# Strided attention on one Trainium2 core: output stored in runs of 2, 4, 4, 4, 4, 4 and 2 groups from one tile, and a TensorE loop of 24 groups

## The chip, the cores and the metric

One core of a Trainium2 chip. The metric is the device time of one execution in microseconds (us). The kernel before took 127.77 us, the median of three runs (127.75 to 128.23).

## What is computed

The inputs Q, K and V have 8 x 12 heads of 1024 positions with 64 numbers each, in float32. Every query attends to every 64th position only, which makes 16 keys and 16 values per head:

```python
attend_positions = np.arange(0, seq, stride)
k = K[:, :, attend_positions, :]
v = V[:, :, attend_positions, :]
scores = np.einsum('bhqd,bhkd->bhqk', q, k) * scale
weights = np.exp(scores - np.max(scores, axis=-1, keepdims=True))
weights = weights / (np.sum(weights, axis=-1, keepdims=True) + 1e-10)
result[:, :, i, :] = np.einsum('bhqk,bhkd->bhqd', weights, v)[:, :, 0, :]
```

Q comes in and the result goes out, 25.2 MB each; of K and V only 0.4 MB each are read.

## The kernel before, in words

The 96 heads are worked in 24 **groups** of four heads. One group is 1 MB of Q: 128 partitions of 8 KB. There are 18 buffers of that size in SBUF, `qn[0]` to `qn[17]`; group g uses `qn[g % 18]`, first for its queries and, once these are used up, for its result (the eviction writes the result over them). In the kernel before, two neighbouring buffers form one tile `pair`.

A group passes these steps, each on one engine:

- `load` (SyncE issues the DMA): Q into the group's buffer.
- `cast` (GpSimd, L305; the first three shared with ScalarE): float32 to bfloat16, into `qb`.
- `transpose` (VectorE, L316): 32x32 blocks of `qb` into `qt`.
- `scores` (TensorE, L324): 16 matmuls against the keys, into PSUM `sc`.
- `largest` (VectorE, L338 and L341): the maximum, and its subtraction, into `low`.
- `raise_` (ScalarE, L346): the exponential, into `ex`.
- `sums` (VectorE, L351 and L354): the sum over the 16 keys and its reciprocal.
- `weights` (GpSimd, L358): `ex` times the reciprocal, into `wt`.
- `turn` (TensorE, L365): four transposes of the weights, into PSUM `tp`.
- `spread` (ScalarE, L377, twice a group): `tp` into the block form `wb`.
- `outputs` (TensorE, L385): eight matmuls with the values, into PSUM `o`, of which there is one.
- `evict` (ScalarE, L403): `o` into the group's buffer.
- `store` (SyncE issues the DMA): the buffer to `out`.

All instructions are recorded first (class `Program`) and then written out in that order, each engine in its own strict order. The order is set by the list `ORDER` with a lag per step: in iteration i come `transpose` of group i, `cast` of i+1, `turn` and `spread` of i-3, `sums` and `weights` of i-2, `outputs` and `evict` of i-4, `largest` and `raise_` of i-1, `scores` of i, and the queue step for group i-5. On GpSimd, then, `cast(i+1)` stands ahead of `weights(i-2)`.

TensorE doesn't get its instructions one by one: it runs a loop of two groups per turn (`pe_stream`), in which step i does `scores(i)`, `turn(i-2)` and `outputs(i-3)`. Gates, semaphores that count up and are set back each turn, hold it: "turned" (VectorE's transposes), "weighted" (GpSimd's weights) and "free" (ScalarE's evictions). Before, the loop has 13 turns, so 26 steps for 24 groups; in the last two there are no more queries, VectorE opens the gate with a small memset (L314), and TensorE repeats score products that nobody reads. The last `outputs(23)` stands behind the loop.

SyncE issues every large DMA, on one hardware queue, and is itself in strict order: a wait at its head holds all that stands behind it. It first issues K, Q of group 0, V, and Q of groups 1 to 17. Then it follows `queue`: with each second group it issues one store of two groups and, at three of these points, the loads of two late groups (18 to 23), which go into buffers whose store must have landed. A store waits for ScalarE's count (`at_ACT`); a load into a used buffer waits for that buffer's store. Groups 22 and 23 are stored singly; the last store stands outside the recorded section, behind its closing handshake of the engines, and GpSimd waits meanwhile for the older stores and clears the semaphores.

The recorded section is opened by one engine, which tells the others to begin: before, SyncE.

Of the kernel before, what the change touches and what calls it, by code (L numbers as in the profile page):

```python
# [42 lines left out]
class Program:  # L43
# [89 lines left out]
    def emit(self, loop):  # L133
# [7 lines left out]
        gates = {name: nc.alloc_semaphore(f"gate_{name}") for name in names}  # L141
        with self.tc.tile_critical(no_gpsimd_drain=True):
# [26 lines left out]
def kernel(  # L169
# [21 lines left out]
    BUFS = 18  # L191
    RUN = 2
    assert NG % RUN == 0 and BUFS % RUN == 0

# [3 lines left out]
    edge = sb.tile([P, 32], FP32, name="edge")  # L198
    pairs = [sb.tile([P, RUN, 32 * D], FP32, name=f"pair{i}") for i in range(BUFS // RUN)]
    qn = [pairs[i // RUN][:, i % RUN] for i in range(BUFS)]  # L200
    k_raw = sb.tile([P, NC, D], FP32, name="k_raw")
# [108 lines left out]
    def transpose(g):  # L310
        k_in = {0: "0", 1: "1"}.get(g)
        words = qt[g % 2].bitcast(I32)
        if g >= NG:
            op("DVE", lambda: nc.vector.memset(edge[:, g - NG : g - NG + 1], 0.0), gate="turned")  # L314
            return
        op("DVE", lambda: nc.vector.transpose(  # L316
# [91 lines left out]
    def send(g, n):  # L408
        return _copy(
            nc,  # L410
            _ap_with(out, [[16 * D, P], [2 * SD, 2 * n], [1, 16 * D]], g * HG * SD),
            _ap_with(qn[g % BUFS], [pairs[0].ap[0], [1, 1], [1, 32 * n * D]]),
        )

    def store(g, n):
        op("SP", lambda: send(g, n), lane=f"out{g % BUFS // n}of{n}",
           reads=[f"qn{i % BUFS}{h}" for i in range(g, g + n) for h in range(2)])
# [33 lines left out]

    turns = (NG + 2) // TURN

    def queue(g):
        if g == NG - 2:
            store(g, 1)
        elif g % RUN == RUN - 1 and g < NG - 1:
            store(g - RUN + 1, RUN)
            late = BUFS + g - 2 * RUN + 1
            if BUFS <= late < NG:  # L460
                for n in range(late, late + RUN):
                    load(n)

    def at(i, stage, lag):
        g = i - lag
        if g in early.get(stage, ()):
            return
        if stage == "transpose" and 0 <= g < NG + 2:
            transpose(g)
        elif stage == "scores" and 0 <= g < NG + 2:  # L470
            scores(g)
# [25 lines left out]
    def pe_stream(sems, gates):  # L497
# [4 lines left out]
        with pe.Fori(0, turns) as turn_:  # L502
# [8 lines left out]
            for name in ("turned", "weighted", "free"):  # L511
                pe.sem_inc(gates[name], -TURN)

    pending, sems = prog.emit(pe_stream)
# [4 lines left out]
    tc.no_sync_barrier()  # L519
    end = send(NG - 1, 1)  # L520
    tc.declare_no_dep(end.ins, landed, reason="waits for the older stores alone")
# [33 lines left out]
```

## Time and profile before

| | us |
|---|---|
| median of three runs | 127.77 |
| the profiled execution's own time | 127.63 |
| its span, first to last instruction | 125.8 |
| ScalarE busy | 93.8 (75%) |
| VectorE busy | 87.1 (69%) |
| GpSimd busy | 75.9 (60%) |
| TensorE busy (matmuls) | 58.1 (46%) |
| bytes moved by DMA | 51.15 MB, mean 406 GB/s over the span |

The span leaves 1.8 us of the execution's own time outside it. Engines are named in the profile as PE (TensorE; PEld are its weight loads), DVE (VectorE), ACT (ScalarE), POOL (GpSimd) and SP (SyncE); SPq is SyncE's sequencer, which issues DMAs. A row of the timeline gives the start in us, the duration in us, engine, line, operation, output<-input and how many instructions are merged. "Landing" of a DMA is the time from its issue until the last of its 16 shares has landed.

### The profile page before, as it was taken

The page shows a single profiled execution, that of the slowest core. Times are in us where ns is not written, and L with a number is a line of the kernel's source. Part 1 is how long each engine was busy: PE and PEld are TensorE (multiplying, and loading weights), DVE is VectorE, ACT ScalarE, POOL GpSimd, SP SyncE. Part 2 cuts the span into 40 slices and gives each one's busy share as a digit, 9 for nine tenths or more (in the row PEclk, how much of TensorE's full clock was granted, in tenths as well). Part 3 has the DMA queues.
Part 4 walks back from the last instruction along what each step waited for, and adds up shares of the span by engine and source line. Part 5 has one row for each costly group of instructions (what it writes and reads, how often), then busy time and mean ns, then how long its engine had stood idle before and what let it go on. Part 6 is the DMA issues. An engine that isn't in the chain of part 4 may idle for free.

```text
span 125.8 us, 2084 instructions
## 1 busy us (share of the span) xinstructions
PE 58.1 (46%) x736; PEld 43.5 (35%) x736; DVE 87.1 (69%) x131; ACT 93.8 (75%) x109; POOL 75.9 (60%) x67
## 2 busy tenths in 40 slices
PE   0007672556489466665555565666656533000000
PEld 0006452445366444443443344444434321000000
DVE  3795879999979899999999999999966100000000
ACT  4266756999888999999999999999999965000000
POOL 5648589999998688889888888879233300000000
PEclk9999999998555999999999999999999975555555
DMA  1998989989899998999999999999999999999991
GB/s 41 425 406 385 490 365 479 448 385 479 365 479 437 406 469 354 422 422 479 417 391 458 422 385 432 464 406 424 417 422 422 427 427 437 427 432 417 406 424 65
DMA packets 6132, 51.15 MB, mean 406 GB/s; under 512 B 3696, under 2 KB 3696, under 8 KB 3696
## 3 DMA queue, kind: packets, MB, share of 16 engines
q1 hardware_dynamic: 6128, 51.12, 96.8%
q14 instruction: 4, 0.03, 0.1%
HBM read 25.95 MB, written 25.17 MB: 406 GB/s over the span
## 4 chain that ended last, share of the span: by engine, by line
ACT 51%; POOL 15%; DVE 7%; DMA 5%; PE 4%; issue 1%; SPq 1%; POOLq 0%
ACT pair L403 28%; ACT wb_all L377 16%; ACT ex L346 7%; POOL qb L305 6%; DMA v_raw<-in_V_dram 5%; POOL wt_all L358 4%; PE o L385 4%; POOL v_all L287 4%; DVE qt L316 3%; DVE total L351 1%; DVE top L338 1%; DVE rec L354 1%; POOL qb L301 1%; SPq L34 1%; DVE low L341 1%
## 5 line engine op out<-in xcount | busy, mean ns | idle before, releaser
L403 ACT COPY pair<-o 128x2048 f32<-128x2048 f32 x24 | 47.9, 1995 | 2.8 <-PE o L385 2.8
L305 POOL CAST qb<-pair 128x2048 bf16<-128x2048 f32 x21 | 39.7, 1892 | 1.5 <-DMA pair<-in_Q_dram 1.5
L385 PE MATMUL o<-v_all,wb_all 128*128 (+1 forms) x216 | 31.6, 295 | 8.2 <-ACT pair L403 8.2
L358 POOL TENSOR_TENSOR wt_all<-ex,rec 128x512 bf16<-128x512 f32 x24 | 25.4, 1058 | 15.4 <-DVE rec L354 15.1
L377 ACT ACTIVATE wb_all<-tp,sel 128x512 bf16<-128x512 bf16 x48 | 33.3, 810 | 0.7 <-PE tp L365 0.6
L316 DVE STREAM_TRANSPOSE qt<-qb 128x1024 int32<-128x1024 int32 x24 | 29.8, 1242 | 1.2 <-POOL qb L305 0.7
L385 PEld LDWEIGHTS o<-v_all,wb_all 128*128 128x128 bf16 x216 | 20.7, 105 | 14.9 <-issue 9.6
L324 PE MATMUL sc<-k_t,qt 128*128 x416 | 19.4, 200 | 12.9 <-DVE qt L316 12.8
L324 PEld LDWEIGHTS sc<-k_t,qt 128*128 128x128 bf16 x416 | 16.9, 103 | 17.5 <-issue 16.6
L365 PE MATMUL tp<-identity,wt_all 128*128 128x128 bf16 x104 | 11.1, 235 | 25.5 <-POOL wt_all L358 25.5
L346 ACT ACTIVATE ex<-low 128x512 f32<-128x512 f32 x24 | 18.3, 764 | 2.5 <-DVE low L341 2.5
L351 DVE TENSOR_REDUCE total<-ex 128x32 f32<-128x512 f32 x24 | 16.3, 678 | 3.9 <-ACT ex L346 3.9
L341 DVE TENSOR_TENSOR low<-sc,top 128x512 f32<-128x512 f32 x24 | 16.6, 691 | 0.8
L365 PEld LDWEIGHTS tp<-identity,wt_all 128*128 128x128 bf16 x104 | 6.4, 103 | 28.3 <-POOL wt_all L358 28.2
L338 DVE TENSOR_REDUCE top<-sc 128x32 f32<-128x512 f32 x24 | 15.2, 632 | 1.3 <-PE sc L324 1.3
L354 DVE RECIPROCAL rec<-total 128x32 f32<-128x32 f32 x24 | 8.5, 353 | 0.8
L287 POOL CAST v_all<-v_raw 32x128 bf16<-32x128 f32 (+1 forms) x12 | 5.2, 431 | 1.5 <-DMA v_raw<-in_V_dram 0.8
L299 ACT CAST qb<-pair 128x1024 bf16<-128x1024 f32 x3 | 3.1, 1045 | 3.1 <-DMA pair<-in_Q_dram 3.1
L301 POOL CAST qb<-pair 128x1024 bf16<-128x1024 f32 x3 | 3.1, 1039 | 3.3 <-DMA pair<-in_Q_dram 3.3
L259 POOL MEMSET v_all<- 128x3456 f32 x1 | 3.0, 2979 | 0.0
L287 ACT CAST v_all<-v_raw 32x640 bf16<-32x640 f32 x4 | 2.9, 722 | 0.0
L250 DVE MEMSET k_t<- 128x1664 uint32 x1 | 1.4, 1445 | 1.9 <-issue 1.9
(15 smaller groups left out, 9.6 us busy)
## 6 DMA issues: line engine op xcount, KB each, us to landing
pair<-in_Q_dram SPq DMA_DIRECT2D x24, 1024.0 KB, 15.0
out_dram<-pair SPq DMA_DIRECT2D x11, 2048.0 KB, 22.8
out_dram<-pair SPq DMA_DIRECT2D x2, 1024.0 KB, 18.7
k_raw<-in_K_dram SPq DMA_DIRECT2D x1, 384.0 KB, 3.9
v_raw<-in_V_dram SPq DMA_DIRECT2D x1, 384.0 KB, 6.8
```

Of the source, the lines that this page charges most:

```text
L305: op("POOL", lambda: nc.gpsimd.tensor_copy(out=b, in_=q), reads=[f"qn{g % BUFS}{h}" for h in range(2)] + apart, writes=[f"qb{g % 2}{h}" fo ...
L316: op("DVE", lambda: nc.vector.transpose(_ap_with(words, [words.ap[0], [1, 2], [D, 16], [2, 32]]), qb[g % 2].bitcast(I32),), reads=[f"qb{g ...
L324: r = nc.tensor.matmul(sc_ps[g % 2][:, 64 * i : 64 * i + 64], lhsT=_ap_with(qt[g % 2], [qt[g % 2].ap[0], [2, P]], extra_offset=2 * P * i + f),
L338: op("DVE", lambda: nc.vector.tensor_reduce(out=m, in_=s, op=ALU.max, axis=mybir.AxisListType.X,), reads=[f"sc{g % 2}"], writes=[f"top{g % ...
L341: op("DVE", lambda: nc.vector.tensor_tensor(out=low, in0=s, in1=m.unsqueeze(2).to_broadcast([P, 32, NK]), op=ALU.subtract,), reads=[f"sc{g ...
L346: op("ACT", lambda: nc.scalar.activation(out=ex[g % 2], in_=low, func=AF.Exp, bias=0.0, scale=scale,), reads=["low"], writes=[f"ex{g % 2}"])
L351: op("DVE", lambda: nc.vector.tensor_reduce(out=total[g % 2], in_=ex[g % 2], op=ALU.add, axis=mybir.AxisListType.X,), reads=[f"ex{g % 2}"] ...
L358: op("POOL", lambda: nc.gpsimd.tensor_tensor(out=wt[g % 2], in0=ex[g % 2], in1=rec[g % 2].unsqueeze(2).to_broadcast([P, 32, NK]), op=ALU.mult,
L365: r = nc.tensor.transpose(tp_ps[g % 2][:, 2 * c : 2 * c + 2].rearrange("p a b -> p (a b)"), wt[g % 2][:, 8 * c : 8 * c + 8].rearrange("p t ...
L377: op("ACT", lambda a=a: nc.scalar.activation(out=wb[g % 2][:, :, 64 * a : 64 * a + 64], in_=tp_ps[g % 2], func=AF.Copy, scale=sel[:, a : a ...
L385: r = nc.tensor.matmul(_ap_with(o_ps, [o_ps.ap[0], [128, 2], [256, 2], [1, D]], extra_offset=512 * c + D * u,), lhsT=wb[g % 2][:, 2 * c + ...
L403: op("ACT", lambda: nc.scalar.copy(to, o_ps.rearrange("p c (b x) -> p c b x", b=2)), reads=["o"], writes=[f"qn{g % BUFS}{n}" for n in rang ...
```

## The change

Four things are changed.

1. **Stores.** The 18 buffers become one tile `q_all`, and the stores are cut as the table `RUNS` says: groups 0-1, 2-5, 6-9, 10-13, 14-17, 18-21, and the last one, 22-23, behind the section. A store of n groups takes 8n KB from each partition, in pieces of 4 KB that lie 512 KB apart in `out`: 2n pieces, so four before and eight now.
2. **Late loads.** A load into a used buffer is now issued behind the first store of `RUNS` that comes after the one that frees it: 18 and 19 behind the store of 2-5, and 20 to 23 behind the store of 6-9.
3. **TensorE.** The loop has 12 turns; the last `turn` and `outputs` steps are written out behind it. The two idle memsets and the two repeats of score products (32 matmuls) are gone.
4. **The opening.** VectorE opens the recorded section.

```diff
-        with self.tc.tile_critical(no_gpsimd_drain=True):
+        with self.tc.tile_critical(sync_engine=mybir.EngineType.DVE, no_gpsimd_drain=True):
...
-    RUN = 2
-    assert NG % RUN == 0 and BUFS % RUN == 0
+    RUNS = {0: 2, 2: 4, 6: 4, 10: 4, 14: 4, 18: 4}
+    ENDS = {g + n - 1: (g, n) for g, n in RUNS.items()}
...
-    pairs = [sb.tile([P, RUN, 32 * D], FP32, name=f"pair{i}") for i in range(BUFS // RUN)]
-    qn = [pairs[i // RUN][:, i % RUN] for i in range(BUFS)]
+    q_all = sb.tile([P, BUFS, 32 * D], FP32, name="q_all")
+    qn = [q_all[:, i] for i in range(BUFS)]
...
-        if g >= NG:
-            op("DVE", lambda: nc.vector.memset(edge[:, g - NG : g - NG + 1], 0.0), gate="turned")
-            return
...
-    turns = (NG + 2) // TURN
+    turns = NG // TURN
+
+    late = list(range(BUFS, NG))
 
     def queue(g):
-        if g == NG - 2:
-            store(g, 1)
-        elif g % RUN == RUN - 1 and g < NG - 1:
-            store(g - RUN + 1, RUN)
-            late = BUFS + g - 2 * RUN + 1
-            if BUFS <= late < NG:
-                for n in range(late, late + RUN):
-                    load(n)
+        if g not in ENDS:
+            return
+        first, n = ENDS[g]
+        store(first, n)
+        while late and late[0] - BUFS < first:
+            load(late.pop(0))
...
             for name in ("turned", "weighted", "free"):
                 pe.sem_inc(gates[name], -TURN)
+        for j in range(2):
+            pe.wait_ge(gates["weighted"], j + 1)
+            turn_products(j).then_inc(done, 1)
+            pe.wait_ge(gates["free"], j + 1)
+            output_products(j + 1, NG + j).then_inc(done, 1)
...
-    end = send(NG - 1, 1)
+    end = send(NG - 2, 2)
```

SyncE's rows behind the first 20 DMAs, before. `pair0` holds groups 0 and 1 (later 18 and 19), `pair1` groups 2 and 3, `pair2` 4 and 5; `at_out0of2` counts the store of `pair0`.

```order
L34 DMA out_0_dram<-pair0_62 128x4x1024 [waits at_ACT]
L34 DMA out_0_dram<-pair1_63 128x4x1024 [waits at_ACT]
L34 DMA pair0_62<-in_Q_dram 128x2048 [waits at_out0of2]
L34 DMA pair0_62<-in_Q_dram 128x2048
L34 DMA out_0_dram<-pair2_64 128x4x1024 [waits at_ACT]
L34 DMA pair1_63<-in_Q_dram 128x2048 [waits at_out1of2]
L34 DMA pair1_63<-in_Q_dram 128x2048
L34 DMA out_0_dram<-pair3_65 128x4x1024 [waits at_ACT]
L34 DMA pair2_64<-in_Q_dram 128x2048 [waits at_out2of2]
L34 DMA pair2_64<-in_Q_dram 128x2048
```

The same place now, down to the section's end; `at_out0` counts the store of groups 0-1 and `at_out2` that of groups 2-5.

```order
L34 DMA out_0_dram<-q_all_62 128x4x1024 [waits at_ACT]
L34 DMA out_0_dram<-q_all_62 128x8x1024 [waits at_ACT]
L34 DMA q_all_62<-in_Q_dram 128x2048 [waits at_out0]
L34 DMA q_all_62<-in_Q_dram 128x2048
L34 DMA out_0_dram<-q_all_62 128x8x1024 [waits at_ACT]
L34 DMA q_all_62<-in_Q_dram 128x2048 [waits at_out2]
L34 DMA q_all_62<-in_Q_dram 128x2048 x3
L34 DMA out_0_dram<-q_all_62 128x8x1024 [waits at_ACT] x3
```

Ahead of load 20 now stand 10 groups of stores on the queue, where before there were 6; it waits for the store of groups 2-5, where before it waited for that of 2-3.

TensorE's rows at the end of the loop and behind it, before: the loop's last transposes and output products, the branch, and `outputs(23)`.

```order
L365 MATMUL tp1_97<-identity_79,wt_all_92 128x128 [waits gate_weighted]
L365 MATMUL tp1_97<-identity_79,wt_all_92 128x128 x3
L385 ISA [waits gate_free]
L385 MATMUL o_98<-v_all_82,wb_all_93 128x2x2x64 x8
L502 REGISTER_ALU
L502 COMPARE_AND_BRANCH
L385 MATMUL o_98<-v_all_82,wb_all_93 128x2x2x64 [waits at_ACT]
L385 MATMUL o_98<-v_all_82,wb_all_93 128x2x2x64 x7
```

And now: behind the branch stand `turn(22)`, `outputs(21)`, `turn(23)`, `outputs(22)` and `outputs(23)`.

```order
L499 REGISTER_ALU
L499 COMPARE_AND_BRANCH
L362 MATMUL tp0_88<-identity_71,wt_all_84 128x128 [waits gate_weighted]
L362 MATMUL tp0_88<-identity_71,wt_all_84 128x128 x3
L382 MATMUL o_90<-v_all_74,wb_all_85 128x2x2x64 [waits gate_free]
L382 MATMUL o_90<-v_all_74,wb_all_85 128x2x2x64 x7
L362 MATMUL tp1_89<-identity_71,wt_all_84 128x128 [waits gate_weighted]
L362 MATMUL tp1_89<-identity_71,wt_all_84 128x128 x3
L382 MATMUL o_90<-v_all_74,wb_all_85 128x2x2x64 [waits gate_free]
L382 MATMUL o_90<-v_all_74,wb_all_85 128x2x2x64 x7
L382 MATMUL o_90<-v_all_74,wb_all_85 128x2x2x64 [waits at_ACT]
L382 MATMUL o_90<-v_all_74,wb_all_85 128x2x2x64 x7
```

Each transposed or output step has the wait that it had in the loop; only the score products between them have left.

More of the change, by code (lines that the diff above doesn't have):

```diff
@@ L411, in send @@
             _ap_with(out, [[16 * D, P], [2 * SD, 2 * n], [1, 16 * D]], g * HG * SD),
-            _ap_with(qn[g % BUFS], [pairs[0].ap[0], [1, 1], [1, 32 * n * D]]),
+            _ap_with(qn[g % BUFS], [q_all.ap[0], [1, 1], [1, 32 * n * D]]),
         )
     def store(g, n):
-        op("SP", lambda: send(g, n), lane=f"out{g % BUFS // n}of{n}",
+        op("SP", lambda: send(g, n), lane=f"out{g % BUFS}",
            reads=[f"qn{i % BUFS}{h}" for i in range(g, g + n) for h in range(2)])
@@ L467, in at @@
             return
-        if stage == "transpose" and 0 <= g < NG + 2:
+        if stage == "transpose" and 0 <= g < NG:
             transpose(g)
-        elif stage == "scores" and 0 <= g < NG + 2:
+        elif stage == "scores" and 0 <= g < NG:
             scores(g)
```

## The prediction

> **What bounds the kernel now.** I read the page's slices first, then the queue's share, then windows by stage, then single DMAs.
>
> ```profile
> span 125.8 us, 2084 instructions
> ...
> ACT  4266756999888999999999999999999965000000
> ...
> DMA  1998989989899998999999999999999999999991
> ...
> q1 hardware_dynamic: 6128, 51.12, 96.8%
> ```
>
> ScalarE is full in the middle and has nothing to do in the last sixth; the DMA row is full from the second slice to the last but one. So the profile's chain of waits, which ends with ScalarE's evictions, tells what the compute is bound by, but compute isn't what the span waits for: the last eviction is over at 106.7 us (104.83 + 1.87, quoted below) and 18 us of stores are still queued. The windows show the rate, in their last two columns (share of the 16 DMA engines, GB/s):
>
> ```profile
> core 0: us, PE busy (x) PEld busy (x) DVE busy (x) ACT busy (x) POOL busy (x), PEclk, DMA share, GB/s
> 0.00:2.00 2.00, 0.00 (x0) 0.00 (x0) 0.10 (x1) 0.68 (x1) 0.57 (x6) 1.00 0.02 4
> 8.00:50.00 42.00, 26.17 (x324) 20.26 (x324) 37.11 (x54) 36.28 (x47) 35.71 (x35) 0.88 1.00 429
> 50.00:85.00 35.00, 20.47 (x280) 15.24 (x280) 34.27 (x52) 35.00 (x41) 29.16 (x21) 1.00 1.01 428
> 107.00:122.00 15.00, 0.00 (x0) 0.00 (x0) 0.00 (x0) 0.00 (x0) 0.00 (x0) 0.50 0.99 421
> 122.00:123.00 1.00, 0.00 (x0) 0.00 (x0) 0.00 (x0) 0.00 (x0) 0.00 (x0) 0.50 0.90 377
> 123.00:124.00 1.00, 0.00 (x0) 0.00 (x0) 0.00 (x0) 0.00 (x0) 0.00 (x0) 0.50 0.30 123
> ```
>
> From 8 to 122 us the engines have no idle time, with loads alone (8 to 50), mixed (50 to 85) or stores alone (107 to 122). The span is therefore the DMA's start (about 2 us), 51.12 MB at 421 to 429 GB/s, and a ragged end: from 122 to 124 the 16 engines stop at different times, over some 2 us. The forecast has to say what the change does to these three, and whether the queue ever runs dry.
>
> **The change part by part.** The sum is made against the profiled execution: 127.63 us, 1.8 us more than its span, and 0.14 below the median of 127.77.
>
> *The bytes* are the same. Only the store's shape can change the rate. Issue times (timeline) and landings (DMA view of the same moment; last number) of four stores and one late load:
>
> ```profile
> 29.60 0.63 SPq L34 DMA_DIRECT2D out_dram<-pair  x1
> out_dram<-pair SPq DMA_DIRECT2D x1, 2048.0 KB, 25.8
> 86.55 0.54 SPq L34 DMA_DIRECT2D out_dram<-pair  x1
> out_dram<-pair SPq DMA_DIRECT2D x1, 2048.0 KB, 23.8
> 100.38 0.54 SPq L34 DMA_DIRECT2D out_dram<-pair  x1
> out_dram<-pair SPq DMA_DIRECT2D x1, 2048.0 KB, 19.7
> 107.28 0.54 SPq L34 DMA_DIRECT2D out_dram<-pair  x1
> out_dram<-pair SPq DMA_DIRECT2D x1, 1024.0 KB, 17.8
> 60.72 0.47 SPq L34 DMA_DIRECT2D pair<-in_Q_dram  x1
> pair<-in_Q_dram SPq DMA_DIRECT2D x1, 1024.0 KB, 12.0
> ```
>
> The store issued at 86.55 lands at 110.35, the next but one (100.38) at 120.08: 9.73 us for two stores of 2 MB, 4.87 us each, which is 431 GB/s (2.097 MB / 4.87). That equals the loads' 429, so there is no fixed cost between queued stores for a larger one to save. A 4 MB store is not in this trace. Bounds: if five of them ran at 429 instead of the 421 of the last stage, 20.97 MB would take 48.9 instead of 49.8 us, a gain of 0.9; if the stores are no better than the neighbouring pair of 2 MB, 0. For a loss I know no reason but the pitch (below); the same 0.9 stands on that side for the range. I take a **gain of 0.2 us**, nearer to the pair of stores, since these are the direct neighbours.
>
> On the DMA's row pitch the Trainium skill speaks against this change: "DMA: Bandwidth & Descriptors", section "Latency and other measured facts", gives 207 GB/s for copies whose rows lie 512 KiB apart. The pieces of a store lie 512 KB apart here, four now and eight after. By that rule 25 MB of stores would already take over 120 us alone, and the trace has 421 to 431 GB/s, so the rule doesn't bind this pattern with four pieces; eight no run here shows yet.
>
> *The opening.* The chain of waits begins so (start, duration, what):
>
> ```profile
> 0.72 0.01 SPq L142
> ...
> 0.80 0.03 SPq L550
> ...
> 0.96 0.43 SPq L236
> ```
>
> SyncE tells the others at 0.72 to begin, passes its own branch at 0.80 and issues K at 0.96. If VectorE tells them instead, SyncE loses one instruction and gains a handover: between -0.08 (the whole step from 0.72 to 0.80) and +0.08. I take 0.
>
> *TensorE's tail* lies under the stores; one of the two repeats of score products that go:
>
> ```profile
> 97.34 0.63 PE L324 MATMUL sc<-k_t,qt 128*128 x16
> ```
>
> Before, the last eviction ends at 106.7, and the last store of 1 MB is issued 0.6 later, at 107.28, and lands at 125.08. At 107.28 the queue still holds the store issued at 100.38, which lands at 120.08; the 32 matmuls and two memsets that go cost nothing while that is so. Without this cover such a step would cost 0.63 us, and both 1.3.
>
> *The late loads* are the part that moves most. Walk along the queue by landings, 4.87 us for 2 MB and 2.44 for a load (1.049 MB at 429): the store of groups 0-1 lands at 55.4 (29.60 + 25.8) as now. Then come the store of 2-5 (9.74: 65.1), loads 18 and 19 (70.0), the store of 6-9 (79.8) and load 20 (82.2). The same walk for the kernel before gives 55.4 + 4.87 + 4.88 + 4.87 + 2.44 = 72.5, and the trace has 72.7 (60.72 + 12.0), so I set load 20 at **82.5**, 21 to 23 at 85, 87.4 and 89.8. GpSimd wants it earlier:
>
> ```profile
> 74.95 1.89 POOL L305 CAST qb<-pair 128x2048 bf16<-128x2048 f32 x1
> 77.39 1.06 POOL L358 TENSOR_TENSOR wt_all<-ex,rec 128x512 bf16<-128x512 f32 x1 [0.55 <-DVE rec L354]
> ...
> 78.50 0.40 PE L365 MATMUL tp<-identity,wt_all 128*128 128x128 bf16 x4 [1.19 <-POOL wt_all L358]
> ...
> 79.64 1.15 ACT wb_all L377 x2
> 80.80 1.75 ACT pair L403
> ...
> 84.24 1.76 ACT pair L403
> ```
>
> `cast(20)` starts at 74.95 now; its load would come 7.6 us later. Behind it in GpSimd's order waits `weights(17)` (77.39), for that `turn(17)` (78.50), and for that `spread(17)` (79.64). Starting cast at 82.55, weights follow at 84.4, turn at 85.5, spread at 85.95: ScalarE, which is otherwise full at 3.44 us a group (80.80 to 84.24), loses **6.3 us**. It can't win them back; the other late loads come 2.4 us apart and are then early enough. So the last eviction ends at 106.7 + 6.3 = 113.0 and the last store is issued at 113.6.
>
> Does that dry the queue? The store of 14-17 needs `evict(17)`, over at 92.3 (84.24 + 1.76 + 6.3), and the queue comes to it at 99.3 (load 23 at 89.5 by the walk, plus 9.74). The store of 18-21 is released where today the store of 20-21 is, at 100.38, plus 6.3: **106.7**. It is wanted when the store of 14-17 ends: 109.0. From issue to first byte it is about 1.1 us (K: issued at 0.96, no bytes but 4 GB/s before 2.00), so bytes flow at 107.8. The 109.0 is the slowest engine's; the ragged end says that the earliest are up to some 2 us ahead, so a few may idle for under 1 us. That shortens only their lead, not the slowest engine's work. The last store (113.6 against 109.0 + 9.74 = 118.7) has 5 us in hand. Cost: **0**, with the margin of 1.2 us against the slowest engine.
>
> Sum: 127.63 - 0.2 + 0 + 0 + 0 = 127.4; set beside the median, which is 0.14 higher, I forecast **127.5 us**.
>
> **The rivals.**
>
> *The queue runs dry ahead of groups 18-21 (slower).* TensorE's clock is the piece that can do it. These rows show half clock (the third number from the end) and what output products then take:
>
> ```profile
> 30.83:41.07 10.24, 7.69 (x74) 5.75 (x70) 8.79 (x13) 9.01 (x10) 9.55 (x9) 0.50 1.04 445
> ...
> 33.50 1.91 PE L385 MATMUL o<-v_all,wb_all 128*128 x8
> ...
> 75.80 1.04 PE L385 MATMUL o<-v_all,wb_all 128*128 x8 [0.35 <-ACT pair L403]
> ...
> 35.45 1.87 ACT L403 COPY pair<-o 128x2048 f32<-128x2048 f32 x1 [0.44 <-PE o L385]
> ...
> 39.38 1.87 ACT L403 COPY pair<-o 128x2048 f32<-128x2048 f32 x1 [0.38 <-PE o L385]
> ...
> 104.83 1.87 ACT L403 COPY pair<-o 128x2048 f32<-128x2048 f32 x1 [1.98 <-PE o L385]
> ```
>
> Output products take 1.91 instead of 1.04 us, and evictions come 3.93 us apart (35.45 to 39.38) instead of 3.44. TensorE would stand idle from 77.3 (78.50 less the 1.19 in its row) to 85.5 while load 20 is late. If it resumes at half clock, the first group loses 0.9 and the next two 0.5 each: up to 1.9 us, and the store of 18-21 is released at 108.6, with bytes at 109.7, against 109.0. That is 0.7 us late for the slowest engine. With load 20 another 0.5 late, 1.2: **128.1 to 128.6** (127.4 plus the loss). It decides from a ScalarE delay of 7.5 us (6.3 + 1.2). For it: the idle time is sure. Against it: the margin and the raggedness.
>
> The Trainium skill, "TensorE: Matmul & The Clock Gate", section "What's actually happening", has the clock halved after an idle window of about 3.4 us and restored after a busy one. The 10.24 us at 0.50 above are three such windows, in a stretch that was far from idle, so the trace agrees on the size of the steps but not on idleness as the only cause. By that rule the clock would be halved here.
>
> *Larger stores are better than I take (faster).* The whole 0.9 of the bound, or a less ragged end: half of the 2 us between 122 and 124. That gives **126.5 to 127.0**. Against it: 4.87 us for 2 MB is already the loads' rate.
>
> *A fixed cost per DMA is saved.* If every DMA cost the 1.1 us that K takes from issue to first byte, six DMAs fewer would save 6.6: **120.8**. The rows contradict it: stores queued behind one another land 4.87 us apart at the loads' rate, with nothing between them. I give it 1 in 100. The Trainium skill's page on DMA, section "Anatomy of one DMA — SWDGE (gpsimd) path", fits 2.0 us per DMA on another issuing path; by that it would be 12 us and 115.4.
>
> *It doesn't do what it says:* if a store of four groups is handled as two of two, nothing changes but the late loads, **127.6**, inside the forecast.
>
> **How the numbers follow.** Forecast, with the last rival in it: 0.66. Queue dry, or the eight pieces slower by the 0.9 (128.5): 0.20. Larger stores or an evener end: 0.13. Fixed cost: 0.01. A change of 0.5% (0.64 us of 127.77) is about what a measurement of this kernel can tell from none: below 127.13 counts as faster, above 128.41 as slower. Of the 0.20, 0.07 stay below 128.41, and of the 0.13, 0.02 above 127.13. So faster 0.12, same 0.75, slower 0.13. The range for 8 in 10 runs from 126.8, most of the gain's bound, to 128.6, the far end of the dry queue.
>
> **What would show it.** Right: DMA share about 1.00 in every stage up to 122 us; load 20 landing at 82 to 83 us; GpSimd idle about 5 us ahead of a cast, ended by a DMA; ScalarE's last eviction ending near 113; neighbouring 4 MB stores landing 9.7 us apart. Wrong: a window between 106 and 111 us with the DMA share well below 1.00 and the end later by as much (the dry queue); 4 MB stores landing 9.5 or 9.9 us apart (their rate); a first load's issue that moved by more than 0.1 us (the opening).

## The result, and the profile after

The kernel after takes **129.17 us**, the median of five runs (128.81 to 129.60), against 127.95 us for the kernel before on the same chip (127.75 to 128.23): **1.010 times as long, 95% interval 1.008 to 1.012**. That is slower than the 127.5 us forecast and outside the forecast's range. Times, ratios and counts here leave disturbed executions out.

Each execution has a time and a span. For the kernel before, over 137 executions beside these experiments, the mean span is 126.10 us, and the time is 1.72 to 1.85 us more (mean 1.78). For the five executions of the kernel after, the mean span is 127.04, and the time is 1.76 to 2.60 more (mean 2.17). So some 0.9 us were lost inside the span and 0.4 us outside. The profiled execution took 129.6 us.

From the page after: the span, TensorE's clock and the DMA engines in 40 slices (3.2 us each), the queue's share, the chain's shares by engine, and the row of GpSimd's casts, with its idle time last.

```profile
span 127.5 us, 1998 instructions
...
PEclk9999999997569999999999999755555595555555
DMA  1999999989999999999999999999999999299795
...
q1 hardware_dynamic: 5264, 51.12, 95.5%
...
DMA 36%; ACT 20%; POOL 14%; PE 13%; DVE 6%; issue 2%; SPq 1%; POOLq 0%; DVEq 0%
...
L305 POOL CAST qb<-q_all 128x2048 bf16<-128x2048 f32 x21 | 39.7, 1891 | 10.1 <-DMA q_all<-in_Q_dram 10.0
```

The row of the casts before:

```profile
L305 POOL CAST qb<-pair 128x2048 bf16<-128x2048 f32 x21 | 39.7, 1892 | 1.5 <-DMA pair<-in_Q_dram 1.5
```

The same bytes as before, but the row of DMA has a hole (the 2) in the slice from 108 to 112 us, the casts wait 10.0 us for loads instead of 1.5, and the clock is at half from the middle of the wait (81.6 us) until long behind it. The windows show the hole (columns as in the prediction; bytes are counted where their transfer starts):

```profile
core 0: us, PE busy (x) PEld busy (x) DVE busy (x) ACT busy (x) POOL busy (x), PEclk, DMA share, GB/s
81.60:102.00 20.40, 13.48 (x116) 10.11 (x116) 13.69 (x20) 13.36 (x15) 12.60 (x9) 0.50 1.01 429
85.00:107.00 22.00, 16.06 (x134) 11.82 (x135) 16.54 (x25) 18.36 (x22) 12.12 (x10) 0.58 1.01 429
107.00:122.00 15.00, 5.20 (x24) 2.70 (x22) 0.47 (x2) 7.31 (x6) 1.06 (x1) 0.50 0.82 351
108.00:109.00 1.00, 0.31 (x4) 0.31 (x4) 0.00 (x0) 1.00 (x1) 0.64 (x1) 0.50 0.31 131
109.00:110.00 1.00, 0.54 (x5) 0.21 (x4) 0.00 (x0) 1.00 (x2) 0.00 (x0) 0.50 0.08 33
110.00:111.00 1.00, 1.00 (x6) 0.71 (x5) 0.00 (x0) 0.88 (x2) 0.00 (x0) 0.50 0.00 0
111.00:112.00 1.00, 0.65 (x4) 0.15 (x1) 0.00 (x0) 0.31 (x1) 0.00 (x0) 0.50 1.21 524
```

Up to 107 us the queue is as full as before. Then the engines run out one by one, from 110 to 111 nothing starts, and between 111.5 and 111.7 all 16 start together, each with 32 KB, which takes it 1.2 us. (A second without a start is no proof by itself: once the engines run in step, a full queue has such seconds too, 119 to 120 for one. The hole is read from the three seconds from 108 to 111 together.) The timeline tells where that comes from (start, duration, engine, what, and in brackets the idle time ahead and what ended it):

```profile
66.00 2.61 SPq L34 DMA_DIRECT2D q_all<-in_Q_dram  x4
...
73.64 1.06 POOL L355 TENSOR_TENSOR wt_all<-ex,rec 128x512 bf16<-128x512 f32 x1 [0.40 <-DVE rec L351]
83.46 1.89 POOL L305 CAST qb<-q_all 128x2048 bf16<-128x2048 f32 x1 [8.76 <-DMA q_all<-in_Q_dram]
85.31 1.06 POOL L355 TENSOR_TENSOR wt_all<-ex,rec 128x512 bf16<-128x512 f32 x1
86.42 0.61 PE L362 MATMUL tp<-identity,wt_all 128*128 128x128 bf16 x4 [9.40 <-POOL wt_all L355]
87.07 1.26 ACT L374 ACTIVATE wb_all<-tp,sel 128x512 bf16<-128x512 bf16 x2 [7.73 <-PE tp L362]
88.77 1.87 ACT L400 COPY q_all<-o 128x2048 f32<-128x2048 f32 x1 [0.44 <-PE o L382]
92.71 1.86 ACT L400 COPY q_all<-o 128x2048 f32<-128x2048 f32 x1 [0.38 <-PE o L382]
...
107.84 1.86 ACT L400 COPY q_all<-o 128x2048 f32<-128x2048 f32 x1 [0.30 <-PE o L382]
110.32 0.54 SPq L34 DMA_DIRECT2D out_dram<-q_all  x1
115.54 1.86 ACT L400 COPY q_all<-o 128x2048 f32<-128x2048 f32 x1 [1.98 <-PE o L382]
```

Load 20, issued at 66.00, lands 17.3 us later, at 83.3 (first row of the next fence). `cast(20)` has waited 8.76 us for it, TensorE 9.40 for the weights behind it, ScalarE 7.73. TensorE resumes at half clock, and the evictions, which before came 3.44 us apart, come 3.94 apart at first. `evict(21)` starts at 107.84 and the store of groups 18 to 21 is issued at 110.32: 9.94 us after the 100.38 of before. By then the store ahead of it, of 14 to 17, issued at 95.13, is at its end (DMA view of the moment of each issue; the last number is the landing):

```profile
q_all<-in_Q_dram SPq DMA_DIRECT2D x1, 1024.0 KB, 17.3
...
out_dram<-q_all SPq DMA_DIRECT2D x1, 4096.0 KB, 15.7
...
out_dram<-q_all SPq DMA_DIRECT2D x1, 4096.0 KB, 11.6
```

95.13 + 15.7 = 110.8, and the store behind it starts to move at 111.5 and lands at 110.32 + 11.6 = 121.9: the queue was dry, for 0.7 us even on the slowest of its 16 engines.

### The profile page after: what moved, and what is told of

Read it like the earlier page. It is cut to its first block, busy times and chain, and to the rows that moved or that the text cites. A ratio compares the mean times of both kernels' runs of the same rounds, so it can differ in the third digit from the quotient of the medians.

```text
span 127.5 us, 1998 instructions
## 1 busy us (share of the span) xinstructions
PE 64.9 (51%) x704; PEld 48.2 (38%) x704; DVE 87.2 (68%) x129; ACT 94.4 (74%) x109; POOL 75.9 (59%) x67
## 3 DMA queue, kind: packets, MB, share of 16 engines
q1 hardware_dynamic: 5264, 51.12, 95.5%
## 4 chain that ended last, share of the span: by engine, by line
DMA 36%; ACT 20%; POOL 14%; PE 13%; DVE 6%; issue 2%; SPq 1%; POOLq 0%; DVEq 0%
DMA out_dram<-q_all 16%; ACT q_all L400 16%; DMA q_all<-in_Q_dram 14%; PE o L382 12%; POOL qb L305 6%; DMA v_raw<-in_V_dram 5%; POOL wt_all L355 4%; POOL v_all L287 3%; DVE qt L313 3%; ACT wb_all L374 3%; ACT ex L343 2%; DVE total L348 1%; PE tp L362 1%; DVE top L335 1%; DVE rec L351 1%
## 5 line engine op out<-in xcount | busy, mean ns | idle before, releaser
L400 ACT COPY q_all<-o 128x2048 f32<-128x2048 f32 x24 | 46.5, 1938 | 5.1 <-PE o L382 5.1
L305 POOL CAST qb<-q_all 128x2048 bf16<-128x2048 f32 x21 | 39.7, 1891 | 10.1 <-DMA q_all<-in_Q_dram 10.0
L382 PE MATMUL o<-v_all,wb_all 128*128 (+1 forms) x216 | 37.6, 333 | 9.1 <-ACT q_all L400 9.1
L374 ACT ACTIVATE wb_all<-tp,sel 128x512 bf16<-128x512 bf16 x48 | 31.9, 752 | 9.1 <-PE tp L362 9.0
L382 PEld LDWEIGHTS o<-v_all,wb_all 128*128 128x128 bf16 x216 | 23.4, 117 | 18.4 <-issue 9.6
L362 PE MATMUL tp<-identity,wt_all 128*128 128x128 bf16 x104 | 12.6, 256 | 30.1 <-POOL wt_all L355 30.1
L321 PEld LDWEIGHTS sc<-k_t,qt 128*128 128x128 bf16 x384 | 18.2, 111 | 15.2 <-issue 13.8
L343 ACT ACTIVATE ex<-low 128x512 f32<-128x512 f32 x24 | 17.2, 718 | 2.1 <-DVE low L338 2.0
L301 POOL CAST qb<-q_all 128x1024 bf16<-128x1024 f32 x3 | 3.1, 1037 | 3.9 <-DMA q_all<-in_Q_dram 3.9
L299 ACT CAST qb<-q_all 128x1024 bf16<-128x1024 f32 x3 | 3.1, 1045 | 2.4 <-DMA q_all<-in_Q_dram 2.3
```

Source lines behind the costliest of these rows:

```text
L305: op("POOL", lambda: nc.gpsimd.tensor_copy(out=b, in_=q), reads=[f"qn{g % BUFS}{h}" for h in range(2)] + apart, writes=[f"qb{g % 2}{h}" fo ...
L321: r = nc.tensor.matmul(sc_ps[g % 2][:, 64 * i : 64 * i + 64], lhsT=_ap_with(qt[g % 2], [qt[g % 2].ap[0], [2, P]], extra_offset=2 * P * i + f),
L343: op("ACT", lambda: nc.scalar.activation(out=ex[g % 2], in_=low, func=AF.Exp, bias=0.0, scale=scale,), reads=["low"], writes=[f"ex{g % 2}"])
L362: r = nc.tensor.transpose(tp_ps[g % 2][:, 2 * c : 2 * c + 2].rearrange("p a b -> p (a b)"), wt[g % 2][:, 8 * c : 8 * c + 8].rearrange("p t ...
L374: op("ACT", lambda a=a: nc.scalar.activation(out=wb[g % 2][:, :, 64 * a : 64 * a + 64], in_=tp_ps[g % 2], func=AF.Copy, scale=sel[:, a : a ...
L382: r = nc.tensor.matmul(_ap_with(o_ps, [o_ps.ap[0], [128, 2], [256, 2], [1, D]], extra_offset=512 * c + D * u,), lhsT=wb[g % 2][:, 2 * c + ...
```

## The experiments

Theory A: the late load dries the queue, by ScalarE's delay and TensorE's half clock together; nothing else costs. Rivals: the 4 MB stores are slower in themselves; the new tail or the opening costs something. All runs at a glance; the ratio is to the kernel before on the same chip, spans and "outside" (time minus span) are means in us, and the last column counts the executions with 2.4 us or more outside:

| run | what it is | ratio, 95% interval | span | outside | 2.4 or more |
|---|---|---|---|---|---|
| before | | 1 | 126.10 | 1.78 | 0 of 137 |
| after | | 1.010 (1.008 to 1.012) | 127.04 | 2.17 | 2 of 5 |
| e11 | after, SyncE opens | 1.0121 (1.0087 to 1.0154) | 127.33 | 2.33 | 4 of 6 |
| e1 | after, loads 20-23 earlier | 1.0053 (1.003 to 1.0076) | 126.38 | 2.21 | 5 of 11 |
| e2 | after, store 18-21 in pairs | 1.0056 (1.0035 to 1.0077) | 126.51 | 2.09 | 4 of 12 |
| e3 | after, TensorE kept busy, straight code | 1.0214 (1.0171 to 1.0257) | 128.84 | 1.77 | 0 of 5 |
| e6 | after, TensorE kept busy, loop | 1.0043 (1.0023 to 1.0062) | 126.63 | 1.80 | 0 of 7 |
| e7 | e1, all stores of 2 MB | 1.0031 (1.0005 to 1.0057) | 125.99 | 2.19 | 5 of 12 |
| e4 | before, late loads as after | 1.001 (0.9999 to 1.0021) | 126.23 | 1.77 | 0 of 12 |
| e8 | before, stores of 1 MB | 1.0132 (1.0115 to 1.015) | 127.67 | 1.82 | 0 of 3 |
| e5 | before, new tail and opening | 1.004 (1.0009 to 1.0072) | 126.17 | 2.17 | 5 of 12 |
| e9 | before, new opening | 1.0013 (0.9988 to 1.0038) | 126.38 | 1.77 | 0 of 12 |
| e10 | before, new tail | 1.0041 (1.0018 to 1.0064) | 126.20 | 2.21 | 5 of 12 |
| e12 | after, old loop | 1.0044 (1.0027 to 1.0061) | 126.66 | 1.78 | 0 of 10 |
| e13 | before, last turn straight | 1.0023 (1.0008 to 1.0039) | 126.25 | 1.82 | 0 of 12 |
| e14 | before, new tail as a loop | 1.0008 (0.9992 to 1.0024) | 126.03 | 1.90 | 0 of 12 |
| e15 | e1, old loop | 1.0034 (1.0012 to 1.0056) | 126.38 | 1.78 | 0 of 12 |
| e16 | after, tail as a loop | 1.003 (1.0002 to 1.0059) | 126.61 | 1.82 | 0 of 12 |
| e17 | e10, padded | 1.0009 (0.9995 to 1.0022) | 126.21 | 1.79 | 0 of 12 |
| e18 | e7, tail as a loop | 0.9998 (0.9983 to 1.0013) | 125.95 | 1.91 | 0 of 12 |

### The dry queue

**e1: loads 20 to 23 ahead of the store of 6 to 9.**

```diff
-        store(first, n)
+        if first == 2:
+            store(first, n)
         while late and late[0] - BUFS < first:
             load(late.pop(0))
+        if first != 2:
+            store(first, n)
```

> The changed kernel with one thing undone: loads 20 to 23 are issued ahead of the store of groups 6-9 instead of behind it. Theory A (late load 20 holds GpSimd, ScalarE and TensorE, TensorE's clock falls to a half, groups 18-21 are evicted late and the DMA queue runs dry for 1.2 us): load 20 lands near 73.5 us, no long wait on GpSimd, evictions 3.42 us apart to the end, store of 18-21 issued near 100.4, DMA share about 1.0 from 107 to 122, time 127.7 to 128.3. Theory B (4 MB stores are themselves slower): still 0.5 or more above the kernel before, 128.5 to 129.2. Theory C (TensorE's written-out tail or the opening by VectorE costs it): unchanged, about 129.2.

The store of 18 to 21 is issued at 100.45, and the queue stays full:

```profile
100.45 0.54 SPq L34 DMA_DIRECT2D out_dram<-q_all  x1
...
107.00:122.00 15.00, 0.00 (x0) 0.00 (x0) 0.00 (x0) 0.53 (x1) 0.00 (x0) 0.50 1.00 428
```

So the late load is what dries the queue. But only half of the loss is back (1.0053): theory A is not the whole.

**e2: the store of 18 to 21 in two pairs.**

```diff
-    RUNS = {0: 2, 2: 4, 6: 4, 10: 4, 14: 4, 18: 4}
+    RUNS = {0: 2, 2: 4, 6: 4, 10: 4, 14: 4, 18: 2, 20: 2}
```

> The changed kernel with the store of groups 18-21 cut into 18-19 and 20-21; load 20 stays late. Theory A: GpSimd's wait of about 9 us, the half clock and a last eviction near 117 stay, but the store of 18-19 is issued near 103, ahead of the queue's end at 109 to 111, so that the gap in the DMA share near 110 is gone: 128.0 to 128.5. Theory B: 4 MB stores up to group 17 remain, so 128.8 to 129.2. If the late eviction itself set the end, and not the empty queue: 129.2.

```profile
101.45 7.88 SPq L34 DMA_DIRECT2D out_dram<-q_all  x2
...
107.00:122.00 15.00, 4.39 (x20) 2.44 (x20) 0.00 (x0) 6.08 (x5) 0.11 (x1) 0.50 0.97 414
```

The load is as late as ever, yet the first pair goes out at 101.45 and bridges the wait for the second; the share rises from 0.82 to 0.97. The hole needs both: a late load, and a store that waits for four groups.

**e3 and e6: TensorE kept busy through the wait**, by repeats of group 19's score products that write the same values again, 17 times in straight code (e3) or 13 times in a loop (e6):

```diff
+                if again and j:
+                    with pe.Fori(0, again):
+                        score_products(j, i)
                 score_products(j, i).then_inc(done, 1)
```

> The changed kernel; while load 20 is late, TensorE repeats the score products of group 19 seventeen more times (about 8 us of matmuls, same result, signalled after the last). Theory A with the clock as a part of it: the granted clock stays 1.0 behind the wait, output products take 1.04 instead of 1.9 us, evictions come 3.44 instead of 3.93 us apart, the store of 18-21 is issued 2 to 2.5 us earlier, near 108, and the time is 128.1 to 128.6. If the half clock doesn't matter, or comes anyway: store near 110.3, 129.2.

> The run that kept TensorE busy, with the thirteen repeats of group 19's score products as a loop of 16 matmuls, since 288 in a row stalled twice for 1.5 and 2.6 us and overran the wait. If the half clock carries a part of the delay: clock 1.0 behind the wait, evictions 3.44 us apart, store of 18-21 issued near 108, time 128.2 to 128.8, as with the last stores cut in two. If not: store near 110.3, 129.2.

e3 missed its aim. In straight code TensorE runs 128 to 131 matmuls and then stands still, waiting for nothing that the profile shows, so that the repeats overran the wait (the last row is the DMA view from 76 to 95 us):

```profile
76.26 3.98 PE L321 MATMUL sc<-k_t,qt 128*128 128x64 bf16 x131
81.71 3.89 PE L321 MATMUL sc<-k_t,qt 128*128 128x64 bf16 x128 [1.47 <-issue]
88.19 1.28 PE L321 MATMUL sc<-k_t,qt 128*128 128x64 bf16 x29 [2.59 <-issue]
...
q8 instruction: 3, 0.05, 1.0%
```

e6 keeps the clock at 1.00 through the wait. But TensorE then still waits 2.68 us for the weights, and from 88 to 94 us the clock is at 0.50 all the same (0.79 on the mean of 85 to 107). The store of 18 to 21 goes out at 109.13 instead of 110.32, and the share is 0.90 instead of 0.82.

```profile
75.88 8.24 PE L321 MATMUL sc<-k_t,qt 128*128 128x64 bf16 x224
86.80 0.40 PE L362 MATMUL tp<-identity,wt_all 128*128 128x128 bf16 x4 [2.68 <-POOL wt_all L355]
...
109.13 7.98 SPq L34 DMA_DIRECT2D out_dram<-q_all  x2
...
76.00:85.00 9.00, 8.12 (x225) 7.49 (x222) 1.78 (x4) 2.91 (x4) 1.17 (x1) 1.00 1.03 437
85.00:107.00 22.00, 13.89 (x136) 9.89 (x136) 16.95 (x26) 19.05 (x23) 13.11 (x11) 0.79 1.00 426
107.00:122.00 15.00, 4.39 (x20) 2.42 (x20) 0.00 (x0) 6.42 (x5) 0.44 (x1) 0.50 0.90 384
```

This agrees with the half clock being part of the hole, but doesn't show it: e16 below, in which nothing was done to the clock, issues the same store at 108.97 with a share of 0.89. That the half clock delays the evictions is read from the trace of the kernel after alone (3.94 us apart instead of 3.44). The fall of the ratio to 1.0043 is not the clock's alone either: 0.4 us of it lie outside the span.

**e4: the late loads alone, in the kernel before.**

```diff
-            late = BUFS + g - 2 * RUN + 1
-            if BUFS <= late < NG:
-                for n in range(late, late + RUN):
-                    load(n)
+            for n in {5: (18, 19), 9: (20, 21, 22, 23)}.get(g, ()):
+                load(n)
```

> The kernel before with one part of the change alone: loads 18 and 19 are issued behind the store of groups 4-5 and loads 20 to 23 behind that of 8-9; all stores keep two groups. Theory A: the wait for load 20 and the half clock come as in the changed kernel (GpSimd idle 8 to 9 us, last eviction near 117), but stores of two groups feed the queue in time: 127.9 to 128.4. If late loads cost the time without large stores: 129 or more.

```profile
L305 POOL CAST qb<-pair 128x2048 bf16<-128x2048 f32 x21 | 39.7, 1890 | 8.7 <-DMA pair<-in_Q_dram 8.7
...
107.00:122.00 15.00, 3.04 (x18) 1.75 (x16) 0.00 (x0) 5.22 (x5) 0.00 (x0) 0.59 0.99 421
```

GpSimd waits 8.7 us for loads and the queue stays full at 0.99: with stores of 2 MB the forecast's "cost 0" holds. (In this execution the clock, too, was back at 1.00 by 91 us.)

### The stores' size

**e7: e1 with each store of four as two of two.**

```diff
-        store(first, n)
+        for k in range(first, first + n, 2):
+            store(k, 2)
```

> Loads 20 to 23 ahead of the store of 6-9, as in the run that undid their lateness (128.68), and each store of four groups issued as two of two, back to back at the same places. If the piece of 32 KB per partition is what costs those 0.7 us: 127.8 to 128.1, and the 16 DMA engines end within 1.8 us of one another. If it is that a store waits for four groups: 128.5 to 128.9.

e7 takes 128.05 us, as the first expectation has it, and what it still loses lies outside the span: its span, 125.99, is no longer than that of the kernel before.

**e8: the kernel before with single stores** (`RUN = 1` instead of 2).

> The kernel before with stores of one group (8 KB per partition), late loads each behind a store as before. If larger pieces make the slowest DMA engine lag more, smaller ones make it lag less: 127.3 to 127.9. If a fixed cost per DMA or per piece counts: 24 instead of 13 stores at 0.05 us (2.49 against 4.87/2 = 2.435 per MB) cost 1.1 us more, 128.5 to 129.2.

```profile
50.00:85.00 35.00, 20.76 (x284) 15.40 (x284) 34.30 (x52) 35.00 (x42) 29.48 (x21) 1.00 1.00 403
107.00:122.00 15.00, 0.00 (x0) 0.00 (x0) 0.00 (x0) 0.00 (x0) 0.00 (x0) 0.50 1.02 427
```

In e8 stores alone run at 427 GB/s, but mixed with loads at 403 instead of 428: smaller stores do cost. From 2 to 4 MB it doesn't go on: the span of e1 and e15 (4 MB) is 0.41 us longer than that of e7 and e18 (2 MB), give or take 0.21, over 23 and 24 executions. The rate of queued stores is hardly it: in the profiled executions, the landings of groups 9 and 21 lie 29.39 and 29.66 us apart in e1 and e15, and 29.38 and 29.49 in e7 and e18. What differs more is the stage with loads: from the landing of load 17 to that of load 23 it takes 29.80 and 29.90 us in e1 and e15, which have one 4 MB store in it, and 29.49 in both e7 and e18. That is one execution of each, so where the 0.4 us arise isn't shown. e7 and e18 also release each pair as soon as its own two groups are evicted (at 94.22 and 101.57 us in e7, where e1 releases four at 100.45); with the queue of e1 full (0.99 from 85 to 107 us, 1.00 from 107 to 122) that should not matter, but no run separates the two.

### The opening and the tail

**e9, e10, e5, e11.** e9 is the kernel before with the opening's line of the change's diff, e10 with the tail's lines, e5 with both; e11 is the kernel after with the opening's line taken back.

> The kernel before with the two other parts alone: TensorE's loop of 24 groups with the last steps written out, and VectorE opening the section; stores and loads as before. If the cost lies in the late loads and the large stores only: 127.7 to 128.1, first issue within 0.05 us of 0.96. If the tail or the opening carries a part of it: 128.3 or more.

> The kernel before with VectorE opening the section and nothing else. The twelve runs with tail and opening together fell into two groups, seven from 127.5 to 128.3 and five from 128.9 to 129.4, which the kernel before doesn't show. If the opening makes the second group: again some of the runs 1 us above the others, mean 128.2 to 128.4. If the tail makes it: all between 127.6 and 128.2.

> The kernel before with TensorE's loop of 24 groups and its written-out tail and nothing else; SyncE opens. If the tail makes the second group of runs: some of them 1 us above the others, mean 128.2 to 128.4. If the opening makes it: all between 127.6 and 128.2.

> The changed kernel with SyncE opening the section as before. If VectorE's opening costs 0.4 us on the mean: 128.5 to 128.9, all runs within 0.6 us. If it costs nothing: 129.0 to 129.3.

The opening can't be told from nothing on the mean (e9), and giving it back to SyncE gains nothing (e11). But 2 of the 12 executions of e9 are 1.2 us above the others, with the time lost inside the span. Over every execution on record of kernels without a hole, 6 of 84 with VectorE's opening have a span of 127.2 us or more, and 3 of 200 with SyncE's. So a cost that comes rarely, of 0.1 us on the mean, isn't excluded. e5, with tail and opening, comes out as the tail alone. The tail alone costs 0.4%, and not inside its span, which is 126.20 against 126.10: in 5 of 12 executions the time is 2.55 to 2.96 us more than the span, in the others 1.73 to 1.90. That is a second cause, of which the forecast knew nothing.

**e12, e15: the old loop of 26 steps** in the kernel after and in e1.

```diff
-    turns = NG // TURN
+    turns = (NG + 2) // TURN
...
-        for j in range(2):
-            pe.wait_ge(gates["weighted"], j + 1)
-            turn_products(j).then_inc(done, 1)
-            pe.wait_ge(gates["free"], j + 1)
-            output_products(j + 1, NG + j).then_inc(done, 1)
```

> The kernel after, but with the kernel before's TensorE loop of 26 steps (two memsets, two repeats of score products; no steps behind the loop but the last output products). Stores, late loads and VectorE's opening stay as after. If the tail costs 0.3 to 0.4% by itself, as the runs with the tail alone suggest, and the dry queue the rest, this gives 1.005 to 1.007 times the time before, with the store of 18 to 21 still issued at about 110 us and the DMA share of the window 107 to 122 still near 0.8. If the tail adds nothing here, because the dry queue realigns the DMA engines and hides what the tail does, it stays at 1.009 to 1.011.

> The kernel after with loads 20 to 23 issued ahead of the store of 6 to 9 and with the kernel before's loop of 26 steps: larger stores and VectorE's opening are what is left of the change. If the tail is what was left of the loss once the loads came early (1.005), this is at 0.999 to 1.002; if stores of 4 MB cost something themselves (their slowest two DMA engines ended at 125.4 to 125.9 us), it stays at 1.003 to 1.005.

Both lose the long times outside the span (0 of 22). e12 came out a little lower than expected, with its hole still there (the store of 18 to 21 at 110.21 us, a share of 0.83). e15 lies within the second expectation: with no hole and no tail, what is left, 4 MB stores and VectorE's opening, is still 0.3% behind.

**e13, e14: straight code or missing work?** e13 is the kernel before with the 13th turn of its loop written out behind a loop of 12; e14 is e10 with the tail as a second loop of one turn.

```diff
+        with pe.Fori(0, 1) as last_:
+            for j in range(2):
...
+            for name in ("weighted", "free"):
+                pe.sem_inc(gates[name], -TURN)
```

> The kernel before, with the last of the 13 turns of TensorE's loop written out straight behind a loop of 12: the same instructions in the same order, memsets and repeats of score products too. If it is the straight code (a longer TensorE program) that costs the 0.3 to 0.4% of the tail, this is at 1.003 to 1.004 with a second group of runs about 1 us later; if it is the work that went (a TensorE that ends earlier, other times of the last evictions), this is at 0.999 to 1.001 with all runs within 0.5 us.

> The kernel before with the new TensorE tail alone, but the tail written as a second loop of one turn instead of straight. The work that went stays away. If the missing work costs the time: 1.003 to 1.004, two groups of runs. If the straight code does: 0.999 to 1.001.

Neither simple answer holds. The same work as a loop costs next to nothing (e14: 1.0008, and 0.1 us more outside the span on the mean), so it isn't the missing work; yet a longer piece of straight code has no long times either (e13: 0 of 12, and most of its 0.2% lies inside the span). What tells the executions apart is in the DMA view. Ten microseconds from 120 us, in 40 slices, of e1, whose profiled execution took 129.3 us with a span of 126.7:

```profile
DMA  9494997949944111110100000000000002000000
...
q1 hardware_dynamic: 101, 1.36, 32.1%
q8 instruction: 1, 0.02, 0.7%
```

And of the kernel before, 127.63 us with a span of 125.8:

```profile
DMA  8999979999954321000000000000000000000000
...
q1 hardware_dynamic: 196, 1.34, 32.0%
```

In e1 one more transfer comes after everything, in the slice from 128.25: 16 KB (0.02 MB) of instructions, on queue q8, 1.8 us after the span's end. e3 shows whose queue this is: it brings three such pieces while TensorE runs straight code. All five profiled executions with 2.4 us or more outside the span (e1, e2, e5, e7, e11) have this transfer behind their end; no other profiled one has, and those with the old loop or the looped tail have none on q8 at all. One doesn't fit: the profiled execution of the kernel after, 2.1 us outside, shows no transfer on q8 either. Where the straight tail got its piece in time, it comes between 108 and 116 us; so in e10, whose profiled execution has 1.8 us outside (its row from 108 to 116 us):

```profile
q8 instruction: 1, 0.02, 0.8%
```

**e16, e17, e18: taking the late piece away.** e16 is the kernel after, e18 is e7, both with the tail as a loop. e17 is e10 with two repeats of score products, which nobody reads, behind the last output products, so that its code is as long as e13's.

```diff
+    def last_products(g):
+        r = output_products(g, g + 3)
+        for j in range(2):
+            score_products(j, NG + j)
+        return r
```

> The kernel after, with the tail behind TensorE's loop written as a second loop of one turn. Theory: part of the loss lies outside the span, because a last 16 KB of TensorE's code is fetched 2 to 3 us after the last store in about 4 of 10 executions of the kernels with the straight tail; as a loop it was fetched late in at most 1 of 12. Then time minus span is 1.7 to 1.9 us in all or nearly all runs, the mean outside the span falls from 2.2 to 1.8 us, and the ratio is 1.006 to 1.008, since the dry queue stays. Rival: the second group of runs comes with the dry queue or the larger stores and stays, 1.009 to 1.011.

> The kernel before with the new tail, and behind the last output products two repeats of score products that nobody reads, so that TensorE's straight code is as long as in the run with the whole last turn written straight. Theory: the code block that the tail's end falls into is then entered long before the end of the program, so its fetch shows before 112 us and no run has 2.4 us or more outside the span; 1.000 to 1.002. Rival: any straight tail brings the second group of runs: 4 of 12 with 2.4 us or more outside, 1.003 to 1.004.

> The kernel after with every known cost taken out: loads 20 to 23 ahead of the store of 6 to 9, each store of four groups as two of two, and the tail as a loop of one turn. If the dry queue, the late code and the 32 KB pieces are all there is, the span is that of the kernel before or up to 0.2 us shorter and the ratio 0.998 to 1.001. If something of the change is left (one tile, the opening), 1.002 to 1.003.

All three lose the long times: 0 of 36 executions with 2.4 us or more, one with 2.32 (e18). e17 has more straight code than e10 and costs less, 1.0009: its piece is asked for earlier, between 104 and 110 us:

```profile
q8 instruction: 1, 0.02, 1.0%
```

e16's ratio, 1.003, is below the 1.006 expected; outside the span it is as expected, and its hole was smaller (its store of 18 to 21 went out at 108.97). e18, with all three costs out, is 0.9998, its window from 107 to 122 is full, and no version tried beats the kernel before by more than can be measured:

```profile
107.00:122.00 15.00, 0.00 (x0) 0.00 (x0) 0.00 (x0) 0.23 (x1) 0.00 (x0) 0.50 1.01 430
```

## Why the prediction was wrong

- **What bounds the kernel** was right: the same 51.12 MB, 429 GB/s from 85 to 107 us, and the part of the loss inside the span that a run could place is a hole in the queue (e1).
- **The late loads, "Cost: 0, with the margin of 1.2 us"**: this step failed. The chain was the right one, link by link, but its sizes were not. Load 20 landed at 83.3, not 82.5, and `spread(17)` started 7.4 us later than before (87.07 against 79.64), not 6.3. The half clock, which the sum left out and gave to a rival, then took some 2.5 us: 0.7 up to the end of the first eviction (88.77 + 1.87 = 90.64 against 80.80 + 1.75 = 82.55, which is 8.1) and 1.9 over the next five (107.84 - 88.77 = 19.1 us, against 5 x 3.44 = 17.2). Release at 110.32 instead of 106.7, against a queue that ends at 110.8 instead of 109.0: with bytes flowing 1.2 us after the issue, at 111.5, the margin of 1.2 us became a lack of 0.7. With e1, e15 (early loads) against the kernel after, e11, e12, e16 (late loads), the hole costs 0.44 us of the span, give or take 0.24. Between kernels with the same tail it is 0.8, give or take 0.5 (the kernel after and e11 against e1), and with the old loop 0.3, give or take 0.4 (e12 against e15). The step also named its cover wrongly: e4 has the same late load and loses 0.1%, since a pair is released two groups earlier. The margin belonged to the store of four.
- **The rival "queue runs dry"** had the mechanism and its turning point (a delay of 7.5 us): the trace passed it with 9.94. By the rule of the Trainium skill, "TensorE: Matmul & The Clock Gate", section "What's actually happening", the clock was to be halved here; the trace agrees (9.40 us idle, and a clock of 0.50 over the window from 81.6 to 102.0). By the same rule of the Trainium skill a sustained busy window of about 3.4 us was to restore it; the trace shows no such return, since TensorE, back at work from 86.4, was busy for 13.48 of the 15.6 us up to 102.0 and stayed at half. Its gaps of 0.6 to 0.8 us in each group may be what kept it there; no run shows that.
- **The bytes, "gain of 0.2 us"**: wrong in sign, inside its bounds of 0.9. The kernels with 4 MB stores have a span 0.41 us longer, give or take 0.21. The argument from neighbouring pairs was nearly right for neighbouring stores (12 MB of them take 29.4 to 29.7 us in e1 and e15, 29.4 to 29.5 in e7 and e18), and had no term for a loss elsewhere. Eight pieces 512 KB apart run at 428 GB/s (e1), no slower than four. The figure that the prediction set beside them didn't describe this pattern: in the Trainium skill, "DMA: Bandwidth & Descriptors", section "Latency and other measured facts", it is for a pitch of 512 KiB from one partition's row to the next, and here neighbouring partitions lie 4 KB apart.
- **TensorE's tail, "lies under the stores"**: true for its work and wrong for its code. I priced the instructions that went and not the place of those that were added: the straight tail costs 0.4 us on the mean, all of it outside the span, where no view that I used could show it.
- **The opening, 0**: right for the first issue, K at 0.96 as before; a rare cost isn't excluded (e9).

Together: 0.44 (hole) + 0.41 (4 MB) + 0.39 (code) = 1.2 us, beside a loss of 1.2 us between the medians and 1.3 between the table's means. That the sum comes so close is luck: each of the first two is known to some 0.2 us, and the 0.41 counts from e7 and e18, whose spans are 0.13 us shorter than that of the kernel before. What stays open: where the kernels with 4 MB stores lose their 0.4 us; why the hole is smaller with the old loop or the looped tail (spans 126.66 and 126.61) than with the straight tail (127.04, 127.33), of which the length of the half clock, different from one execution to the next, may be the cause; and what decides in which executions the code comes late.

## What to carry to other kernels

A store that waits for more groups is released later, and that eats the very margin that a later load needs: price the two together, from the release of the last piece and not of the first. When a chain on the edge of drying a queue contains a TensorE wait of several microseconds, put the half clock into the sum and not into a rival. And look at the time outside the span of many executions, since straight code at the end of a program can cost there, with every instruction inside the span on time.

## What was not expected of the hardware

- TensorE's code comes in pieces of 16 KB on a queue of its own. Straight code stood still for 1.47 and 2.59 us after 131 and 128 matmuls (e3), while 224 matmuls in a loop ran without a gap (e6). The Trainium skill, "Runtime: NRT & Kernel Launch", section "Instruction fetch mechanics", has blocks of 16 KiB or 256 instructions, and calls the cost of crossing into the next one mostly hidden. The size agrees (128 matmuls with their 128 weight loads are 256); hidden it was not, neither in e3 nor at the program's end, where it came late in five profiled executions. Of the 70 executions with the tail that ends this way, 30 have 2.4 us or more outside the span, 0.6 to 1.3 us more than the kernel before.
- The 16 DMA engines, which end a full queue some 2 us apart, start together after a hole: in the kernel after, all 16 start between 111.5 and 111.7 us.
- Stores of 1 MB between loads bring the queue down to 403 GB/s, stores of 2 MB leave it at 428.
